# Taking the input tiles of the projection turned as well as plain, in a hybrid streaming encoder layer

## The chip, the cores and the metric

The kernel runs on one core of a Trainium2 chip. Its metric is the device time of one launch in microseconds (us). Time before: 3008.1 us, the median of three runs (3006.89 to 3008.73). The profile is of one execution, taken by the hardware profiler.

A core has a tensor engine (PE; its weight loads are listed as PEld), a vector engine (DVE), a scalar engine (ACT), a general engine (POOL), and a queue that issues most transfers (SP). Each works through its own queue in order, and they meet through semaphores. PE writes only to PSUM; DVE and ACT read it; POOL works on SBUF alone.

## The reference, cut to what matters

One layer on 2048 prompt rows and 128 sample rows of width 1024, 17 tiles of 128 rows in all, and on 256 memory rows (two tiles):

```
def rmsnorm(x, g):
    return x * rsqrt(mean(x * x, axis=-1) + EPS) * g

mk, mv = rmsnorm(mem, g_mem_kv) @ w_mk, rmsnorm(mem, g_mem_kv) @ w_mv   # memory keys and values
h = rmsnorm(x, g_mix_pre)
q, k, v, u_val, u_gate = split(h @ w_in)        # 1024 -> 5 x 512
att = band_attention(q, k, v);  c = conv_module(u_val * sigmoid(u_gate))
x = x + rmsnorm(concat(att, c) @ w_out, g_mix_post)
x = x + rmsnorm(memory_attention(rmsnorm(x, g_mem_pre), mk, mv), g_mem_post)
x = x + rmsnorm((silu(h2 @ w_gate) * (h2 @ w_up)) @ w_down, g_ffn_post)   # h2 = rmsnorm(x, g_ffn_pre)
```

The change concerns the first norm of x and the norm of the memory: a scale per row (a token), a weight per column (a channel), and then a product that contracts over the channels, for which the channels have to lie on the partitions.

## The kernel before, in words

All products are of float32 numbers cut into a high and a low half in a rounded format (`hi` is the cast, `lo` what is left), and each product is done as three: high by high, high by low, low by high (lines 288 to 290, `mm3`). So each weight tile of 128 x 1024 is loaded by SP (line 277), cast by ACT (line 281), and subtracted by DVE or POOL (line 283), through three load buffers and four pairs of halves.

The stages in order of time:

- *Memory stage* (`phase_mem`, up to about 111 us). Both memory tiles are normed, turned and split. Then, for the eight blocks of w_mk, 24 products of 256 columns each (the K product), with a pair of transposes per block to bring the result back (line 413); then a fold of w_mq into the keys, eight weights, 32 sums of six products, each sum copied out of PSUM by DVE (line 448) (called f1 below); then the eight blocks of w_mv (the V product); and a fold of w_mo into the values, 16 sums of six products of 512 columns, copied out at line 462 (f2).
- *Projection* (`phase_proj`, up to about 560 us). The 17 tiles are taken in three groups (`GROUPS`) of two sub-blocks of up to three tiles; per sub-block `norm_sub` norms, turns and splits its tiles into one of three pairs of buffers (`hh`, `hl`). Per group PE makes the gate and value inputs of the convolution (384 columns, line 510), then v (256 columns, line 660), then k and q. DVE runs the depthwise convolution between its other work (line 542), and POOL one quarter of it (line 552). The last products are followed by attention, the output projection, the memory attention and the feed-forward part, which the change leaves alone.

A tile's norm (`prenorm_halves`) is, before: SP loads the tile with rows on the partitions (line 500, or 385 for the memory), ACT squares it and sums each row (line 313), POOL makes the scale (lines 305 and 306), DVE multiplies the tile by the row's scale and the weight, which lies spread over all partitions (line 331), PE turns the eight blocks of 128 x 128 by transposes into two PSUM tiles (line 335), ACT casts each to the high half (line 337), and DVE subtracts (line 338). The tiles' load buffers (`xt`) are two. For the memory, PE spreads the weight over the partitions by two products with ones (line 398), among transposes of the identity that do nothing else (line 395).

The order on each engine isn't written out: a scheduler sets it when the program is built, from the order of the code, priorities and its own estimate of the times, and it lets a norm of a later tile pass other work where its buffers are free. So the norms of the projection's first tiles lie among the products of the memory stage. Most of PSUM is four sum tiles (`mm`) and two for transposes (`tr`).

## Time and profile before

| | us |
|---|---|
| median of three runs | 3008.1 |
| span of the profiled execution | 3000.1 |
| median less span | 8.0 |
| PE busy in the span | 2949.2 |
| DVE busy | 2134.6 |
| ACT busy | 1360.3 |
| POOL busy | 1416.7 |

The profile gives no launch time for the profiled execution itself; its span is 3000.1 us, from the first instruction to the last, and 8.0 us is what the median of the runs has beyond it. A row of a timeline has the start, the duration, the engine, the line of the kernel, the operation, what is written and read, and, in brackets, how long the engine was idle before and what it waited for. A row of a group has the busy time, the mean duration in ns, and the idle time ahead of it. Busy times of PE overlap, since its products are pipelined: the step from one start to the next tells what one costs.

### The profile page before, as it was taken

To read this page: it belongs to the slowest core of one execution; us is meant where nothing else is said; L and a number is where in the kernel's file an instruction comes from. 1 tells how busy PE (TensorE), PEld (TensorE's weight loads), DVE (VectorE), ACT (ScalarE), POOL (GpSimd) and SP (SyncE) were. 2 spreads that over 40 slices of the span, in tenths; PEclk is the share of its full clock that TensorE was granted. 3 is DMA by queue.
4 is the path that set the end of the run, shared out by engine and by line. 5 is a ranking of instruction groups with operands and counts; after the bars stand their busy time and mean duration, and the time that the engine had idled before them with its cause. 6 is when DMAs were issued, how large, how long until landed. Compare 5 with 4: busy or idle time off the path is not lost.

```text
span 3000.1 us, 46145 instructions
## 1 busy us (share of the span) xinstructions
PE 2949.2 (98%) x16940; PEld 2714.6 (90%) x16940; DVE 2134.6 (71%) x3090; ACT 1360.3 (45%) x2731; POOL 1416.7 (47%) x1338
## 2 busy tenths in 40 slices
PE   9999999999999999999999999999999999999998
PEld 9999999989997887887888999999999999888777
DVE  6687886968776466435358888888788998555666
ACT  5535455668883344323334333433344444433433
POOL 0267496721123244136357565446555775424413
PEclk9999999989999999999999999999999999999999
DMA  7645253664435456323246333544334336756664
GB/s 278 246 138 185 88 170 108 201 213 168 155 138 175 169 199 205 105 87 133 88 163 222 116 137 124 196 153 152 134 134 157 142 140 205 256 176 215 217 223 148
DMA packets 197552, 499.57 MB, mean 167 GB/s; under 512 B 19334, under 2 KB 84750, under 8 KB 188485
## 3 DMA queue, kind: packets, MB, share of 16 engines
q1 hardware_dynamic: 182397, 427.01, 41.9%
q0 software_dynamic: 14928, 69.61, 6.2%
q8 instruction: 133, 2.18, 0.3%
q14 instruction: 94, 0.77, 0.1%
HBM read 365.45 MB, written 141.81 MB: 169 GB/s over the span
## 4 chain that ended last, share of the span: by engine, by line
PE 38%; DMA 4%; issue 3%; DVE 3%; POOL 3%; ACT 0%; SPq 0%; DVEq 0%; POOLq 0%; ACTq 0%
PE psb L290 12%; PE psb L288 12%; PE psb L289 12%; DMA sbf<-in_w_down_dram 2%; POOL sbf L1569 1%; PE psb L296 1%; DMA sbf<-x 1%; PE psb L1424 1%; DMA sbf<-hn 0%; DVE sbr L1639 0%; DVE sbr L1447 0%; POOL sbf L346 0%; DVE sbr L1573 0%; DMA sbf<-in_w_gate_dram 0%; DVE sbx L1447 0%
## 5 line engine op out<-in xcount | busy, mean ns | idle before, releaser
L288 PE MATMUL psb<-sbr 128*128 128x384 f32 (+3 forms) x2808 | 941.7, 337 | 4.1 <-DVE sbx L676 1.6
L289 PE MATMUL psb<-sbr 128*128 128x384 f32 (+3 forms) x2356 | 804.6, 342 | 0.4 <-DVE sbr L338 0.3
L290 PE MATMUL psb<-sbr 128*128 128x512 f32 (+3 forms) x1848 | 633.1, 344 | 4.3 <-DVE sbr L1639 4.1
L288 PEld LDWEIGHTS psb<-sbr 128*128 128x128 f32 x2808 | 529.2, 189 | 34.6 <-ACT sbr L1638 2.8
L290 PE MATMUL psb<-sbr,sbx 128*128 128x384 f32 (+2 forms) x1484 | 475.8, 321 | 0.0
L289 PEld LDWEIGHTS psb<-sbr 128*128 128x128 f32 x2356 | 443.9, 188 | 27.1 <-DVE sbr L1427 0.7
L290 PEld LDWEIGHTS psb<-sbr 128*128 128x128 f32 x1848 | 347.9, 188 | 34.9 <-DVE sbr L1639 8.2
L296 PE MATMUL psb<-sbr 128*128 128x512 f32 x1200 | 295.3, 394 | 1.9 <-ACT sbr L1317 1.1
L1447 DVE TENSOR_TENSOR sbr<-sbf,sbr 128x512 fp32r<-128x512 f32 x258 | 262.7, 1021 | 38.8 <-ACT sbr L1446 37.9
L1446 ACT CAST sbr<-sbf 128x512 fp32r<-128x512 f32 x258 | 159.2, 620 | 277.4 <-PE psb L289 229.3
L290 PEld LDWEIGHTS psb<-sbr,sbx 128*128 128x128 f32 x1484 | 279.6, 189 | 0.2
L542 DVE SCALAR_TENSOR_TENSOR psb<-sbf,psb 128x768 f32<-128x768 f32 (+1 forms) x290 | 264.3, 911 | 6.1
L296 PEld LDWEIGHTS psb<-sbr 128*128 128x128 f32 x1200 | 222.2, 189 | 47.6 <-ACT sbr L1317 1.3
L1639 DVE TENSOR_TENSOR sbr<-sbf,sbr 128x384 fp32r<-128x384 f32 (+2 forms) x242 | 168.1, 717 | 99.2 <-ACT sbr L1638 98.0
L283 POOL TENSOR_TENSOR sbx<-sbf,sbr 128x1024 fp32r<-128x1024 f32 (+1 forms) x62 | 155.0, 2501 | 84.8 <-ACT sbr L281 81.0
L1638 ACT CAST sbr<-sbf 128x384 fp32r<-128x384 f32 (+2 forms) x242 | 112.4, 483 | 174.1 <-PE psb L289 149.8
L1569 POOL TENSOR_TENSOR sbf<-sbf 128x512 f32<-128x512 f32 x77 | 106.5, 1390 | 168.7 <-DMA sbf<-in_w_down_dram 167.1
L552 POOL TENSOR_TENSOR flexb<-flexb,flexb 128x128 f32<-128x128 f32 (+1 forms) x180 | 168.9, 939 | 25.4 <-ACT flexb L551 15.1
L288 PE MATMUL psb<-sbr,sbx 128*128 128x384 f32 (+1 forms) x524 | 170.6, 327 | 1.8 <-ACT sbx L1446 1.1
L1446 ACT CAST sbx<-sbf 128x512 fp32r<-128x512 f32 x153 | 94.7, 620 | 163.4 <-PE psb L289 143.4
L1447 DVE TENSOR_TENSOR sbx<-sbf,sbx 128x512 fp32r<-128x512 f32 x153 | 153.4, 1004 | 17.0 <-ACT sbx L1446 16.8
L1441 POOL TENSOR_TENSOR sbf<-sbf 128x512 f32<-128x512 f32 x66 | 97.5, 1477 | 107.2 <-DVE sbr L1447 50.7
(350 smaller groups left out, 6281.5 us busy)
## 6 DMA issues: line engine op xcount, KB each, us to landing
af<-flexb SPq DMA_DIRECT2D x33, 1344.0 KB, 5.8
sbf<-in_w_down_dram SPq DMA_DIRECT2D x154, 256.0 KB, 3.5
sbf<-in_w_gate_dram SPq DMA_DIRECT2D x66, 512.0 KB, 3.3
sbf<-in_w_up_dram SPq DMA_DIRECT2D x66, 512.0 KB, 3.5
sbf<-af SPq DMA_DIRECT2D x85, 384.0 KB, 4.3
sbf<-x SPq DMA_DIRECT2D x49, 512.0 KB, 3.8
sbf<-in_w_in_dram SPq DMA_DIRECT2D x48, 512.0 KB, 3.8
sbr<-ks POOLq DMA_DIRECT2D x16, 1024.0 KB, 8.6
```

What stands on the lines that cost most here:

```text
L283: self.lo_engine.tensor_tensor(lo[:, c], wf[:, c], hi[:, c].bitcast(F32), ALU.subtract)
L288: nc.tensor.matmul(ps, lh, rh, start=start, stop=False, **kw)
L289: nc.tensor.matmul(ps, lh, rl, start=False, stop=False, **kw)
L290: nc.tensor.matmul(ps, ll, rh, start=False, stop=stop, **kw)
L296: nc.tensor.matmul(y[o], l, r[:, o * 512:(o + 1) * 512], start=start and x == 0, stop=stop and x == 2)
L542: nc.vector.scalar_tensor_tensor(acc if w < CW - 1 else o, src(w), cwt[:, j, w:w + 1], acc, ALU.mult, ALU.add)
L552: nc.gpsimd.tensor_tensor(o, o, v, ALU.add)
L1446: nc.scalar.copy(hs[j][:, :], src[j])
L1447: nc.vector.tensor_tensor(ls[j][:, :], src[j], hs[j][:, :].bitcast(F32), ALU.subtract)
L1569: nc.gpsimd.tensor_tensor(acc[:, :], acc[:, :], q[:, :], ALU.add if s > 0 else ALU.subtract)
L1638: nc.scalar.copy(ch[:, m], a[:, x, m])
L1639: nc.vector.tensor_tensor(cl[:, m], a[:, x, m], ch[:, m].bitcast(F32), ALU.subtract)
```

## The change

The host now also passes x and the memory turned: for each tile, channels on the partitions, in eight blocks of 128 tokens. `prenorm_halves` is replaced by two functions, and the two norm weights come in with channels on the partitions, one number for each partition and block (`gT`).

```
--- before
+++ after
-    def prenorm_halves(self, pool, pspool, xt, gbc, hi, lo):
+    def row_scale(self, pool, natural, r):
         nc = self.nc
-        r = self.rms(pool, xt[:, :])
-        nc.vector.scalar_tensor_tensor(xt[:, :], xt[:, :], r[:, :], gbc[:, :], ALU.mult, ALU.mult)
+        xt = self.t(pool, [P, D], F32, "xt")
+        nc.sync.dma_start(xt[:, :], natural)
+        junk = self.t(pool, [P, D], BF16, "junk")
+        nc.scalar.activation(junk[:, :], xt[:, :], AF.Square, accum_out=r)
+        nc.gpsimd.tensor_scalar(r, r, 1.0 / D, EPS, ALU.mult, ALU.add)
+        self.last_pow = nc.gpsimd.tensor_tensor(r, r, self.mhalf[:, 0:1], ALU.pow)
+
+    def norm_turned(self, pool, pspool, turned, r, gT, hi, lo):
+        nc = self.nc
+        xT = self.t(pool, [P, KC, P], F32, "xT")
+        nc.sync.dma_start(xT[:, :, :], turned)
+        nc.gpsimd.tensor_tensor(xT[:, :, :], xT[:, :, :], gT[:, :].unsqueeze(2).to_broadcast([P, KC, P]), ALU.mult)
+        ps = self.t(pspool, [P, P], F32, "tr")
+        nc.tensor.transpose(ps[:, :], r.to_broadcast([P, P]), self.ident[:, :])
         for k0 in range(0, KC, 4):
-            ps = self.t(pspool, [P, 4, P], F32, "tr")
-            for k in range(4):
-                nc.tensor.transpose(ps[:, k, :], xt[:, (k0 + k) * P:(k0 + k + 1) * P], self.ident[:, :])
             sl = slice(k0, k0 + 4)
-            last = (nc.scalar.copy(hi[:, sl, :], ps[:, :, :]),
-                    nc.vector.tensor_tensor(lo[:, sl, :], ps[:, :, :], hi[:, sl, :].bitcast(F32), ALU.subtract))
+            nc.vector.tensor_tensor(xT[:, sl, :], xT[:, sl, :], ps[:, :].unsqueeze(1).to_broadcast([P, 4, P]), ALU.mult)
+            last = (nc.scalar.copy(hi[:, sl, :], xT[:, sl, :]),
+                    nc.vector.tensor_tensor(lo[:, sl, :], xT[:, sl, :], hi[:, sl, :].bitcast(F32), ALU.subtract))
...
-        for o in range(3):
-            with self.tc.issue_after(event.ins) if event else ExitStack():
-                for _ in range(WARM[o]):
-                    nc.tensor.transpose(warm[:, :], self.ident[:, :], self.ident[:, :])
-            if o < 2:
-                oc = slice(o * 512, (o + 1) * 512)
-                event = nc.tensor.matmul(gbc[:, oc], ones[:, :], gain[:, oc], start=True, stop=True)
+        for _ in range(WARM):
+            nc.tensor.transpose(warm[:, :], self.ident[:, :], self.ident[:, :])
...
             for i, t in enumerate(sub):
-                xt = self.t(pool, [P, D], F32, "xt", 2)
-                nc.sync.dma_start(xt[:, :], self.rows("x", t))
-                self.prenorm_halves(pool, ps_tr, xt, gbc, hh[:, :, i * P:(i + 1) * P], hl[:, :, i * P:(i + 1) * P])
+                self.norm_turned(pool, ps_tr, A["xT"][t], rx[:, t:t + 1], gT, hh[:, :, i * P:(i + 1) * P], hl[:, :, i * P:(i + 1) * P])
...
+        rx = self.t(pool, [P, NPT + 1], F32, "rx")
+
+        def scales(subs):
+            for sub in subs:
+                for t in sub:
+                    self.row_scale(pool, self.rows("x", t), rx[:, t:t + 1])
+
+        scales(GROUPS[0])
         nxt = [norm_sub(GROUPS[0][0]), norm_sub(GROUPS[0][1])]
         conv_halo()
+        scales(GROUPS[1])
...
+            if gi == 1:
+                scales(GROUPS[2])
```

So the plain tile now serves only for the row's scale, one column of a small tile (`rx`) per tile, taken for whole groups ahead. The turned tile is multiplied by the weight on POOL; one transpose of the scale, spread over 128 columns, puts the scales of the tile's tokens along the free dimension on all partitions; and DVE multiplies both halves of the tile by it, reading the scales from PSUM. ACT and DVE split the tile as before, but out of SBUF. The space of the old weight (4 KB) and one of the two plain buffers went to two buffers for turned tiles; plain tiles of the projection now pass through one buffer. For the memory tiles, the products with ones go, and the twelve transposes of the identity stand together. The intermediate `yf` of the memory stage moved to another place.

More of the change, by code (lines that the diff above doesn't have):

```diff
@@ L44 @@
 LATE = 5
-WARM = (6, 0, 6)
+WARM = 12
 HP = 100
@@ L174, in early @@
                    .lay(sbF, 2, ("thx", 2, 1), ("zx", 2, 2), ("xnx", 2, 2))
-                .lay(sbF, 44.75, ("us", 5.75, 1), ("cwt", 0.484375, 1), ("cvec", 0.0625, 1), ("half", 0.0625, 1))
+                .lay(sbF, 44.75, ("us", 5.75, 1), ("cwt", 0.484375, 1), ("cvec", 0.0625, 1), ("half", 0.0625, 1), ("gT", 0.03125, 1), ("rx", 0.09375, 1))
                    .lay(fb, 0, ("ct", 3, 5), ("bst", 0.03125, 2), ("bmv", 0.03125, 2), ("ss", 0.03125, 6),
@@ L469, in phase_proj @@
         big = [P, KC, 3 * P]
-        gbc = self.gain(pool, "g_mix_pre", "gbc")
+        gT = self.t(pool, [P, KC], F32, "gT")
+        nc.sync.dma_start(gT[:, :], A["g_mix_preT"])
         cwt = self.t(pool, [P, 4, CW], F32, "cwt", 1)
@@ L1682, in layout, with turned @@
     o["mem_prompt"] = i["mem_prompt"].reshape(NM, D)
+    def turned(x):
+        return x.reshape(-1, P, KC, P).transpose(0, 3, 2, 1)
+    o["xT"] = turned(np.concatenate([o["x_prompt"], o["x_sample"]]))
+    o["mem_promptT"] = turned(o["mem_prompt"])
+    for n in ("g_mix_pre", "g_mem_kv"):
+        o[n + "T"] = i[n].reshape(KC, P).T
     o["cache_att_k"] = i["cache_att_k"].reshape(DEC_B, PAST, 512)
@@ L1704, in layout @@
     o["w_down"] = i["w_down"].reshape(NF, P, D)
-    for n in ("g_mix_pre", "g_mix_post", "g_mem_pre", "g_mem_post", "g_mem_kv", "g_ffn_pre", "g_ffn_post"):
+    for n in ("g_mix_post", "g_mem_pre", "g_mem_post", "g_ffn_pre", "g_ffn_post"):
         o[n] = i[n].reshape(D)
```

22 lines of the change are left out of this document (8 added, 14 removed).

## The prediction

> **What bounds the kernel now.** I read the page first, then stretches of the first 490 us (all that the change touches), then PE's waits there.
>
> ```profile
> PE 2949.2 (98%) x16940; PEld 2714.6 (90%) x16940; DVE 2134.6 (71%) x3090; ACT 1360.3 (45%) x2731; POOL 1416.7 (47%) x1338
> ```
> ```profile
> 13.00:37.50 24.50, 24.31 (x204) 24.31 (x205) 17.85 (x26) 14.57 (x30) 0.00 (x0) 1.00 0.69 243
> 37.50:60.30 22.80, 22.80 (x192) 22.74 (x191) 18.81 (x37) 8.32 (x12) 0.00 (x0) 1.00 0.92 315
> 60.30:86.00 25.70, 25.70 (x218) 25.70 (x217) 18.25 (x29) 15.31 (x30) 2.32 (x4) 1.00 0.71 248
> 86.00:111.00 25.00, 25.00 (x124) 20.70 (x123) 23.15 (x34) 14.34 (x25) 5.52 (x6) 1.00 0.90 324
> 111.00:150.00 39.00, 38.65 (x237) 37.93 (x236) 19.49 (x23) 18.62 (x36) 16.67 (x17) 1.00 0.54 201
> 150.00:490.00 340.00, 338.45 (x2192) 337.31 (x2191) 261.99 (x322) 160.32 (x261) 236.36 (x162) 1.00 0.43 143
> ```
> ```profile
> PE psb L288 <- DVE sbx L676: 1.6, 2, 0.8
> PE psb L335 <- DVE sbr L338: 0.5, 1, 0.5
> ```
>
> Columns of the stretches: length, then busy time (and instructions) of PE, PEld, DVE, ACT, POOL, then granted clock, DMA share, GB/s. The rows are the memory stage (K product, f1, V product, f2), the start of the projection, and the projection. PE hardly pauses from 13 us on, at clock 1.00, so a product that leaves PE's queue shortens the run by its issue time, unless its place becomes a wait. Two stretches have little room: DMA is at 0.92 in f1, and DVE is busy 23.15 of 25.0 us in f2.
>
> Sums go against the profiled execution: span 3000.1 us, 8.0 us under the 3008.1 us median of the runs; I keep those 8.0.
>
> **The change part by part.**
>
> *Transposes.* Per tile eight go and one comes: 152 become 19.
>
> ```profile
> 114.37 0.33 PE L290 MATMUL psb<-sbr,sbx 128*128 128x384 f32 x1
> 114.54 0.34 PE L288 MATMUL psb<-sbr 128*128 128x384 f32 x1
> 114.72 1.03 PE L335 MATMUL psb<-ident,sbf 128*128 128x128 f32 x8
> 115.51 0.42 PE L289 MATMUL psb<-sbr 128*128 128x384 f32 x1
> 115.77 0.34 PE L290 MATMUL psb<-sbr,sbx 128*128 128x384 f32 x1
> ```
>
> Products issue every 0.17 us. From 114.54 to 115.77 two issue steps (0.35) and the block of eight passed: 1.23 - 0.35 = 0.88 us, 0.11 each. Seven fewer per tile save 0.77 us; for the 17 tiles of x **13.1 us**. The memory's two tiles lie ahead of the first product and are counted below.
>
> *Start.* Two gain products (L398) and the scale of the whole row go; two turned loads and two POOL products come.
>
> ```profile
> 4.43 1.06 ACT L313 ACTIVATE sbf<-sbf 128x1024 bf16<-128x1024 f32 x1 [2.43 <-DMA sbf<-in_mem_prompt_dram]
> 5.83 1.06 ACT L313 ACTIVATE sbf<-sbf 128x1024 bf16<-128x1024 f32 x1 [0.25 <-DMA sbf<-in_mem_prompt_dram]
> 12.45 1.37 DVE L338 TENSOR_TENSOR sbr<-psb,sbr 128x512 fp32r<-128x512 f32 x2 [0.97 <-ACT sbr L337]
> 13.19 0.38 PE L289 MATMUL psb<-sbr 128*128 128x256 f32 x1 [0.34 <-DVE sbr L338]
> ```
> ```profile
> L346 POOL TENSOR_TENSOR sbf<-sbf 128x1024 f32<-128x1024 f32 x16 | 40.4, 2522 | 11.7 <-DVE sbf L345 11.7
> ```
>
> Natural loads land 1.4 us apart; without the gain's issue in front (0.4) at 4.0 and 5.4, so the first turned tile at about 7.0 (estimate, one more step of 1.4 and the small gain). POOL multiplies two tiles, 2.5 us each by L346, the same size: 9.5, 12.0. DVE then does the second tile's two halves (1.3) and three subtractions up to the one that the second kind of product waits for (2.0): 15.2, against 13.19. I take **+2.0**, with ends +1.0 (turned tile at 6.0) and +3.5 (at 8.5). The first weight lands later too, behind two more loads, but POOL takes its low half only after the two tiles, so it is not later than that.
>
> *DVE, ACT, POOL per tile.*
>
> ```profile
> L338 DVE TENSOR_TENSOR sbr<-psb,sbr x38: 676/683/692, 9.9 to 465.0; 128x512 fp32r<-128x512 f32 x38
> L331 DVE SCALAR_TENSOR_TENSOR sbf<-sbf,flexb x17: 1275/1285/2864, 70.9 to 425.0; 128x1024 f32<-128x1024 f32 x17
> ```
>
> DVE had 1.28 + 2 x 0.68 = 2.65 us; now four of 0.68, 2.7 us: nothing. ACT keeps one square and two casts. POOL gains 2.5 us per tile, 28 us for tiles 6 to 16, on top of 236 in 340 us: hidden, as weights are prepared up to four ahead. If that cover went, each of these low halves would come 2.5 us late.
>
> L331 reads SBUF twice and was stretched to 2.86 us; L338 reads PSUM and never was, and its successor reads SBUF twice. The Trainium skill, SBUF — State Buffer, section Who interferes with whom, says that such a DVE operation and a POOL operation exclude each other for the whole instruction; by the stretched row the trace agrees. By the unstretched rows the extra cost is nothing; by that rule 22 subtractions in the projection would each wait about 1 us on average (estimate), 22 us on a DVE that idles 78 us there, and I would add 1 us: 3002.6 in place of 3001.6.
>
> *Projection.* The 0.35 us before 150 us and the 1.6 us behind L676 may go, or grow through a DVE queue that now also waits for POOL's product. I take **+1.0**, ends -1.5 and +3.
>
> *f1: a new wait in PE's queue.* The scale's transpose writes one of two PSUM halves, which is free when DVE has multiplied the tile before last. In the order in which the changed program is built, the tiles pass as 1, 3, 5 and then 0, 2, 4; PE meets the transpose of tile 5 in f1, after 19 of its 32 sums; it waits for DVE on tile 3, whose turned load goes into tile 1's buffer, freed after the 7th sum.
>
> ```profile
> 42.42 0.42 DVE L448 COPY flexb<-psb 128x256 f32<-128x256 f32 x1 [0.29 <-PE psb L290]
> 43.14 0.43 DVE L448 COPY flexb<-psb 128x256 f32<-128x256 f32 x1 [0.29 <-PE psb L290]
> ```
> ```profile
> 92.44 0.40 SPq L500 DMA_DIRECT2D sbf<-in_x_prompt_dram  x1
> 97.61 1.06 ACT L313 ACTIVATE sbf<-sbf 128x1024 bf16<-128x1024 f32 x1 [3.75 <-DMA sbf<-in_x_prompt_dram]
> 98.57 0.19 ACT L313 ACTIVATION_READ_ACCUMULATOR sbf<-sbf 128x1 f32 x1
> 100.22 0.33 SPq L500 DMA_DIRECT2D sbf<-in_x_prompt_dram  x1
> 107.69 1.06 ACT L313 ACTIVATE sbf<-sbf 128x1024 bf16<-128x1024 f32 x1 [0.94 <-DMA sbf<-in_x_prompt_dram]
> ```
>
> A sum takes 0.72 us. Counted from f1's start: buffer free at 7 x 0.72 = 5.0, plus about 2.3 for tile 1's halves in DVE's queue, 7.3; landing 5.2 later (92.44 to 97.61), 12.5; POOL 2.5, 15.0; DVE 1.3, 16.3. PE is there at 19 x 0.72 = 13.7. **+2.5**; ends 0 (landing within 2.6) and +5 (landing 7.5, as from 100.22 to 107.69). Behind it stand PE's whole queue and, in DVE's, four evictions.
>
> *f2.* PE sheds 24 transposes (2.6 us) and would leave after 22.4 us, but DVE's work there stays near 23.2, and tile 2's turned load, needed for the first projection, now starts only when tile 0 is done in the same stage. **+1.0**, ends 0 and +4.
>
> *Queues and DMA.* SP issues 19 more loads of 512 KB at 0.33 us: hidden. Natural loads of tiles 0 to 5 now stand between the weight loads of the K product and f1, through one buffer: each waits in SP's queue for ACT's square of the one before, and two or three weights pass between two of them. PE uses a weight in 24 products of 0.12 (13.53 to 13.65) and one pair of transposes, about 3.1 us, two in 6.2. A round is landing + 1.06 + 0.19 + about 0.3 for the handoff: 6.0 to 6.8 with landings of 4.4 to 5.2.
>
> ```profile
> 13.53 0.28 PE L288 MATMUL psb<-sbr 128*128 128x256 f32 x1
> 13.65 0.28 PE L289 MATMUL psb<-sbr 128*128 128x256 f32 x1
> 18.11 1.23 DVE L283 TENSOR_TENSOR sbx<-sbf,sbr 128x1024 fp32r<-128x1024 f32 x1 [1.35 <-ACT sbr L281]
> ```
> ```profile
> sbf<-in_w_mqT_dram SPq DMA_DIRECT2D x8, 512.0 KB, 4.4
> ```
>
> So it just keeps up. The lead: the fourth weight is ready at 19.3 (18.11 + 1.23) and used at 13.2 + 3 x 3.1 = 22.5, 3.2 us; its load waits for the first weight's low half, which POOL ends 3.2 us later than now (15.0 against 11.8, estimate), and PE starts 2.0 later: about 2 us are left. I take **0.1**, ends 0 and the fourth case below.
>
> *Sum.* 13.1 - (2.0 + 1.0 + 2.5 + 1.0 + 0.1) = 6.5: span 2993.6, median **3001.6 us**.
>
> **The rivals.**
>
> *A, the forecast:* the saving, half given back: 3001.6, own range 2998 to 3003.
>
> *B, covered:* nothing is late behind the start (PE paused nowhere in the memory stage, which speaks for it): 13.1 - 2.0 = 11.1, 2997.0. Against it: the queue order above.
>
> *C, given back:* loads land in 7.5 us, not 5.2, with DMA at 0.9 and nine more loads before 60 us. The wait in f1 grows by 2.3, tile 2 comes 2.3 later: 3006.2. For it: 107.69; against it: 97.61 and the median 4.4.
>
> *D, slower:* the chain of natural loads starves the weights. The opening stretch had a 512 KB load that landed in 8.5 us.
>
> ```profile
> sbf<-in_g_mix_pre_dram SPq DMA_DIRECT2D x1, 512.0 KB, 8.5
> ```
>
> With that the round is 10.05, 3.85 more than PE's 6.2, in five rounds 19 us, less the lead of 2: 3001.6 + 17 = 3018.6. It turns the sign past the bound (12.5 above the forecast) when a round exceeds 9.1 us, a landing of 7.6.
>
> The Trainium skill, DMA: Bandwidth & Descriptors, section Anatomy of one DMA, fits a transfer as 2.0 us and its bytes at 436 GB/s: 3.2 us for 512 KB, so by that rule a round of 4.8 never starves PE and B is right; the landings of this trace are longer, and they decide.
>
> **How the numbers follow.** A measurement tells about 0.2% (6 us) from no change. A 0.36, B 0.12, C 0.32, D 0.20. Faster by more than 0.2%: A and B less the upper edge of A, 0.46; within: 0.34; slower: D, 0.20. Range 2995 to 3013: B's case and 2 us of before's small waits below, C and the beginnings of D above.
>
> **What would show it.** Transposes at the new line: 19, and about 0.1 us each between products. First steady product near 15.2 us. PE's waits before 130 us: one on DVE's scale product of 2 to 3 us in f1, about 1 at the end of f2, none on ACT's weight cast. DVE's subtraction with minimum 0.68 and a longer maximum. From 600 us on PE's stretches as before, 6 us earlier. Wrong if PE waits for weights in the K product (D), if the wait in f1 is under 0.5 (B) or over 4 (C), or if the projection pauses for more than 3 us.

## The result, and the profile after

The changed kernel took 3024.5 us (median of 4 runs, 3023.2 to 3027.5), the kernel before 3007.5 us beside it (median of 4, 3006.8 to 3008.7): a ratio of 1.0067, 95% interval 1.0048 to 1.0087. It is slower; 3001.6 was forecast, with 3013 as the upper end.

The profiled execution of the changed kernel has a span of 3023.5 us and took 3025.3, so only 1.8 us lie around a span. The 8.0 us that the prediction put around the span of the kernel before were mostly something else: by the same 1.8 us its profiled execution took some 3001.9 us (estimate), less than any of the four runs beside the changed kernel. So the two profiles differ by 23.4 us and the medians by 17.0; the some 6 us between are that one execution of the kernel before, not the change. A second profile of the kernel before (an experiment, below) has a span of 3000.5 at a time of 3002.3, on a chip where the median of that kernel is 3002.0; so whether the first was a short execution or on such a chip is not known.

First row: the page of the changed kernel, busy time and instructions per engine. Then its waits of PE in the first 620 us (us in total, times, longest; a short one at the very start is left out).

```profile
PE 2941.6 (97%) x16803; PEld 2706.8 (90%) x16803; DVE 2148.2 (71%) x3108; ACT 1359.8 (45%) x2731; POOL 1451.7 (48%) x1357
```
```profile
PE psb L288 <- ACT sbr L348: 6.2, 1, 6.2
PE psb L288 <- DVE sbx L686: 6.0, 3, 4.7
PE psb L289 <- DVE sbx L283: 3.7, 1, 3.7
PE psb L344 <- POOL sbf L335: 3.0, 2, 2.1
PE psb L344 <- DVE sbf L347: 1.9, 1, 1.9
...
PE psb L288 <- ACT sbr L281: 1.0, 1, 1.0
PE psb L289 <- DVE sbr L349: 0.7, 1, 0.7
```

The profile counts 137 instructions of PE less (133 transposes and two products went) and 7.6 us less of busy time; the time went into waits that the kernel before did not have or had shorter: the first product (L348), v's evictions (L686), the weight split on DVE at the end of f2 (L283), a tile's transpose in f1 (L347), and the transposes of the two memory tiles ahead of the first product (L335, at 6.3 and 7.7 us).

Where the time went is read from the same landmarks in both traces, in us from the start of the span: the starts of the first and last eviction of f1 (line 448) and of the last of f2 (line 462), the first glu (the first gated input of the convolution, which DVE writes at line 625 before and 633 after), the last subtraction for k in the projection (line 714 before, 724 after; so the projection runs on to some 615 us, not 560), the last score product of attention, and the end. The third row is the difference; the forecast is the sum of the prediction's own steps up to there, with 0.77 us per tile taken off where the kernel before turned its tiles (5 of 17 ahead of the first glu, 12 behind it).

| | f1 first | f1 last | f2 last | first glu | projection's end | last score | end |
|---|---|---|---|---|---|---|---|
| before | 38.6 | 61.5 | 111.2 | 120.3 | 614.6 | 896.4 | 3000.1 |
| after | 44.8 | 71.3 | 125.8 | 134.3 | 625.1 | 920.4 | 3023.5 |
| later by | +6.2 | +9.8 | +14.6 | +14.0 | +10.5 | +24.0 | +23.4 |
| forecast | +2.0 | +4.5 | | +1.6 | -6.5 | -6.5 | -6.5 |

So of the 30 us between forecast and end 17 lie ahead of the projection's end, and 13.5 inside attention, whose code is the same in both.

**The start.** PE's rows of the changed kernel at its first products, then two stretches of it (columns as in the prediction; the x number is the instructions), then POOL and DVE ahead of them.

```profile
14.30 0.58 PE L288 MATMUL psb<-sbr 128*128 128x256 f32 x1 [6.16 <-ACT sbr L348]
15.85 0.58 PE L288 MATMUL psb<-sbr 128*128 128x256 f32 x1 [0.96 <-ACT sbr L281]
17.14 0.58 PE L289 MATMUL psb<-sbr 128*128 128x256 f32 x1 [0.71 <-DVE sbr L349]
```
```profile
17.00:22.00 5.00, 4.86 (x22) 4.86 (x23) 2.96 (x4) 0.80 (x2) 4.03 (x3) 1.00 0.89 341
22.00:27.00 5.00, 5.00 (x41) 5.00 (x41) 2.78 (x4) 3.62 (x7) 2.84 (x4) 1.00 0.62 228
```

```profile
9.13 3.75 POOL L342 TENSOR_TENSOR sbf<-sbf 128x1024 f32<-128x1024 f32 x2 [1.52 <-DMA sbf<-in_mem_promptT_dram]
14.11 3.58 DVE L349 TENSOR_TENSOR sbr<-sbf,sbr 128x512 fp32r<-128x512 f32 x4
```

POOL waited for the first turned tile up to 9.13 us, and of DVE's four subtractions from 14.11 on the first took 1.77 us, beside a weight split of POOL. PE stood still for 6.2 us, and then made 22 instructions in 5 us where later it makes 41: its products step by 0.21 us up to 22.4 us and by 0.12 behind that. (The clock column says 1.00 there because the profile's first record of the clock is later, at 22.6 us; in the kernel before it is at 12.2 us.)

**The end of f2.** DVE and POOL of the changed kernel.

```profile
113.95 1.78 DVE L349 TENSOR_TENSOR sbr<-sbf,sbr 128x512 fp32r<-128x512 f32 x1
115.66 3.36 DVE L283 TENSOR_TENSOR sbx<-sbf,sbr 128x1024 fp32r<-128x1024 f32 x1
```
```profile
112.92 2.27 POOL L342 TENSOR_TENSOR sbf<-sbf 128x1024 f32<-128x1024 f32 x1 [5.96 <-DVE flexb L462]
115.15 2.78 POOL L283 TENSOR_TENSOR sbx<-sbf,sbr 128x1024 fp32r<-128x1024 f32 x1
```
```profile
119.08 0.79 PE L289 MATMUL psb<-sbx,sbr 128*128 128x512 f32 x1 [3.69 <-DVE sbx L283]
```

A weight split takes DVE 1.21 to 1.23 us elsewhere; this one ends 1.1 us after POOL's split ends at 117.93, and the subtraction ahead of it 0.55 us after POOL's product ends at 115.19. So each looks as if it stood still until POOL was done, which is tested below. PE waits 3.69 us for it. In the kernel before no split on DVE took more than 1.23 us.

**The clock.** Stretches of the changed kernel around that wait and around the 4.7 us wait in the v products.

```profile
118.10:124.90 6.80, 5.82 (x14) 4.57 (x15) 5.66 (x9) 1.42 (x3) 4.72 (x2) 0.50 0.77 258
125.00:131.00 6.00, 6.00 (x35) 5.83 (x35) 3.42 (x3) 2.10 (x2) 4.24 (x2) 1.00 0.99 363
220.50:227.30 6.80, 6.06 (x28) 6.06 (x29) 3.35 (x6) 1.81 (x4) 4.64 (x3) 0.50 0.66 212
227.40:233.40 6.00, 5.70 (x47) 5.46 (x47) 6.00 (x9) 4.33 (x8) 2.51 (x2) 1.00 0.49 161
```

With each of the two waits PE's granted clock falls to 0.50 for 6.8 us; half of the 5.8 and 6.1 us in which PE worked at it, some 3 us, is what that costs (estimate). In the kernel before it is 1.00 from its first record to 623 us. The wait of 1.9 us in f1 has no such stretch behind it. The Trainium skill, TensorE: Matmul & The Clock Gate, section Part 1: The HAM clock gate, says that an idle window of some 3.4 us halves the clock and that a busy one gives it back, in windows that run freely. The traces agree on the windows: in each profile of this study all changes of the clock lie on a grid of 3.41 us (stretches of 3.4, 6.8, 10.2 us). They do not agree that a whole window has to be idle. Up to 615 us, over the 17 profiles, half clock followed each of the 23 grid intervals at full clock in which PE stood idle for 2.0 us or more, and 2 of the 25 with 1.2 to 1.9 us. So a wait's place on the grid decides, and not its length alone. Two of the kernels below show it, the best version and the one with attention's loads behind the last norm, with PE's row behind the wait and then the clock:

```profile
111.33 0.61 PE L290 MATMUL psb<-sbx,sbr 128*128 128x512 f32 x1 [2.10 <-DVE sbx L284]
111.60:115.00 3.40, 3.40 (x9) 2.62 (x9) 3.40 (x7) 0.39 (x1) 2.94 (x2) 0.50 0.72 245
```
```profile
120.28 0.50 PE L289 MATMUL psb<-sbx,sbr 128*128 128x512 f32 x1 [3.67 <-DVE sbx L283]
118.40:125.20 6.80, 4.53 (x20) 3.49 (x21) 6.80 (x10) 3.32 (x4) 5.60 (x4) 1.00 0.77 270
```

The first wait, 2.1 us, lies in one interval and is followed by half clock; the second, 3.7 us, falls into two intervals, 1.8 and 1.9 us, and is followed by none.

**Attention.** The kernel before, then the changed one: the store of the third of five late convolution norms on SP, POOL's loads for head 1 (4 MB), and ACT at the fifth norm, which needs the third one's buffer (two buffers).

```profile
637.75 0.32 SPq L578 DMA_DIRECT2D cs<-sbf  x1
...
638.73 0.64 POOL L853 DMA_DIRECT2D sbr<-qs  x1
639.37 1.22 POOL L855 DMA_DIRECT2D sbr<-ks  x2
640.41 0.73 POOL L856 DMA_DIRECT2D sbr<-vs  x1
...
641.70 1.51 ACT L573 ACTIVATE sbf<-psb,sbf 128x128 f32<-128x128 f32 x4 [0.56 <-PE psb L570]
```
```profile
648.35 0.64 POOL L863 DMA_DIRECT2D sbr<-qs  x1
648.99 1.21 POOL L865 DMA_DIRECT2D sbr<-ks  x2
650.03 0.72 POOL L866 DMA_DIRECT2D sbr<-vs  x1
...
650.31 1.79 SPq L577 DMA_DIRECT2D cs<-sbf  x2
...
663.95 1.50 ACT L572 ACTIVATE sbf<-psb,sbf 128x128 f32<-128x128 f32 x4 [9.58 <-DMA cs<-sbf]
...
665.51 2.08 PE L901 MATMUL psb<-ident,flexb 128*128 128x128 f32 x7 [7.84 <-ACT sbf L572]
```

In the kernel before the store leaves 1.0 us ahead of the 4 MB, and the fifth norm does not wait for it 4.0 us later (its landing is not recorded; that of the second store, 3.5 us earlier, took 2.2 us). In the changed kernel it leaves 2.0 us behind the first of these loads and lands in 13.6. ACT waits 9.58 us with casts behind it in its queue, PE 7.84 us, and the clock is at 0.50 for 23.9 us there instead of 20.5. Softmax number 10 of attention (from 0) comes 1.5 us earlier than before, counted from the first score product, number 12 comes 14.6 us later: 16.0 us at one place.

### The profile page after: what moved, and what is told of

The parts are those of the page before. It is cut to its first block, busy times and chain, and to the rows that moved or that the text cites. A ratio compares the mean times of both kernels' runs of the same rounds, so it can differ in the third digit from the quotient of the medians.

```text
span 3023.5 us, 45902 instructions
## 1 busy us (share of the span) xinstructions
PE 2941.6 (97%) x16803; PEld 2706.8 (90%) x16803; DVE 2148.2 (71%) x3108; ACT 1359.8 (45%) x2731; POOL 1451.7 (48%) x1357
## 4 chain that ended last, share of the span: by engine, by line
PE 40%; DMA 3%; DVE 3%; POOL 3%; issue 2%; ACT 1%; SPq 0%; DVEq 0%; POOLq 0%; ACTq 0%
PE psb L290 12%; PE psb L289 12%; PE psb L288 12%; PE psb L296 2%; DMA sbf<-in_w_down_dram 1%; POOL sbf L1579 1%; DMA sbf<-x 1%; PE psb L1434 1%; DVE sbr L1649 1%; POOL sbf L357 0%; DVE sbr L1457 0%; DVE sbf L374 0%; DMA sbf<-in_w_gate_dram 0%; DVE sbr L1583 0%; DVE sbx L1457 0%
## 5 line engine op out<-in xcount | busy, mean ns | idle before, releaser
L283 POOL TENSOR_TENSOR sbx<-sbf,sbr 128x1024 fp32r<-128x1024 f32 (+1 forms) x62 | 148.7, 2399 | 52.4 <-ACT sbr L281 51.1
L1457 DVE TENSOR_TENSOR sbx<-sbf,sbx 128x512 fp32r<-128x512 f32 x153 | 153.7, 1006 | 15.4 <-ACT sbx L1456 15.2
```

What stands on the lines that cost most here:

```text
L283: self.lo_engine.tensor_tensor(lo[:, c], wf[:, c], hi[:, c].bitcast(F32), ALU.subtract)
L1457: nc.vector.tensor_tensor(ls[j][:, :], src[j], hs[j][:, :].bitcast(F32), ALU.subtract)
```

## The experiments

The theory after these readings, T in the expectations: the loss is the start (first product later, then half clock), DVE's standstill beside POOL, the v products' wait, and one late store in attention, each with half clock behind it. Its rivals, R, stand with each run. Ratios are to the kernel before beside it; a difference of 0.001 is 3 us. "Later by" is against the first profile of the kernel before.

**How far one program's profiles differ.** The kernel before again, unchanged.

> The kernel before once more, unchanged, for a second profile: how far stages differ between executions of one program. If the stages up to the first glu differ by under 1 us between its two profiles, lags of 2 us and more there belong to the change; attention's length (279.3 us in the first profile from the first to the last score product) tells what of the 13 us lost there can be chance.

Every landmark up to the projection's end lies within 0.1 us of the first profile, the last score 2.2 us later, the end 0.4. For the changed kernel that is not so. Three of the kernels below (attention's loads behind the last norm, a third buffer, the bias tables earlier) have its order on every engine, the first two up to attention, the third up to 129 us. Their lags beside its own, and the start of the steady run of products:

| | steady run from | f1 first | f1 last | f2 last | first glu | projection's end |
|---|---|---|---|---|---|---|
| the changed kernel | 17.1 | +6.2 | +9.8 | +14.6 | +14.0 | +10.5 |
| loads behind the last norm | 16.0 | +4.4 | +10.7 | +13.8 | +13.7 | +12.6 |
| a third buffer | 16.1 | +4.8 | +8.8 | +11.5 | +11.1 | +7.3 |
| bias tables earlier | 16.3 | +5.2 | +10.3 | +15.1 | | |

So a difference of under 2 us at f1, or of 3 to 5 us up to the projection's end, between two kernels with turned tiles can be that of two executions. The wait of 3.7 us at the end of f2 is in all four, with the same durations of 1.78 and 3.36 us on DVE; the half clock with it lasts 6.8, 0, 0 and 3.4 us.

**Attention's loads behind the last norm.**

```diff
-            self.late_event = self.last_pow
...
-            nc.vector.scalar_tensor_tensor(z[:, :, :], th[:, :, :], 1.0, z[:, :, :], ALU.add, ALU.mult)
+            self.late_event = nc.vector.scalar_tensor_tensor(z[:, :, :], th[:, :, :], 1.0, z[:, :, :], ALU.add, ALU.mult)
```

> The changed kernel, with one instruction as the event behind which attention's loads of head 1 (q, k and v, 4 MB on POOL's queue) are issued: the last convolution norm's final multiply by DVE in place of its rstd on POOL, so that no store of a convolution norm shares the DMA engines with those 4 MB. Theory T (the 13 us lost in attention are one late store: it landed after 13.6 us instead of 2.2, held ACT by 9.6 us and PE by 7.8 us, and PE then ran at half clock): the PE wait on ACT of 7.8 us is gone, the long stretch at half clock shrinks by some 7 us, the time falls by 8 to 11 us, to 3013 to 3017. Rival R (the loss only moves on: head 1's loads now come later and its first score waits for them, or the next buffer does): another PE wait of 5 us or more between 630 and 720 us, time 3021 to 3027.

3023.7 us, ratio 1.0052 (1.0038 to 1.0067). PE's 7.8 us wait went to 1.5, but ACT still waited 4.2 us for the store, which now stood beside two loads of 512 KB, and from softmax 10 to 12 it lost 9.2 us instead of 16.0. T's place was right, its gain was not reached: the edit took away one neighbour of the store, not the wait for it.

**A third buffer.** What the store holds up is a buffer, so one more was given (2 KB that were free).

```diff
-                   .lay(sbF, 2, ("thx", 2, 1), ("zx", 2, 2), ("xnx", 2, 2))
+                   .lay(sbF, 2, ("thx", 2, 1))
+                   .at("zx", 2, (sbF, [4, 6, 0])).lay(sbF, 8, ("xnx", 2, 2))
```

> The changed kernel with three buffers in place of two for the result of the late convolution norms (zx), so that the fifth norm need not wait for the store of the third, which lands late when attention's 4 MB for head 1 are being fetched. Between the 10th and the 12th softmax of attention the changed kernel lost 16 us against the kernel before, and so did every kernel in which ACT waited 7.7 us or more for that store (the changed one, the one with earlier bias tables, the memory half alone, the product on ACT); the four without that wait lost under 3.5 there. Theory T: ACT's wait for the store is gone, the loss at the 12th softmax is under 4 us, the time is 8 to 12 us below the changed kernel's: ratio to the kernel before 1.001 to 1.003. Rival R (the planner's order, not the store, sets that place): the loss stays over 8 us, ratio 1.004 to 1.007.

Ratio 1.0035 (1.0022 to 1.0049), 0.0032 or 9.6 us below the changed kernel's; span 3013.6, 9.9 less. PE's waits between 620 and 700 us in that kernel, longest group first:

```profile
PE psb L885 <- DVE flexb L797: 4.0, 4, 1.6
PE psb L570 <- DVE sbf L566: 1.4, 1, 1.4
PE psb L902 <- ACT sbf L573: 1.2, 1, 1.2
```

The wait on ACT is 1.2 us instead of 7.8, and from softmax 10 to 12 the loss is 2.7 instead of 16.0. T holds for that place: its loss is the wait for the store. Not all of the 13.5 us in attention go with it. Of the 9.9 us of span 3.2 lie ahead of the projection's end, where the order is the changed kernel's; from there to the last score this kernel still loses 7.0 us, 6.6 less. The wait is not tied to the turned tiles: of the kernels with two buffers, the four in which ACT waited 7.7 us or more for it lost 15.6 to 16.8 us at this place (the changed kernel, and of the kernels below the ones with the bias tables earlier, the memory half alone and the weight on ACT), those in which it waited 3.2 and 4.2 us at a time lost 8.2 and 9.2 (the scaled tile in PSUM, attention's loads behind the last norm), and those in which it waited 1.3 us or less lost 2.7 to 3.0 (PE kept busy, eight transposes, the projection half alone). As far as these kernels show, the order that the scheduler plans for attention decides, and it moves with changes ahead of it; why it comes out one way or the other was not tried.

**The bias tables earlier.** The call moves from behind the four glu blocks of group 0 into the first.

```diff
+                if gi == 0 and j == 0:
+                    self.bias_tables(Region().lay(fa, 0, ("fb", 3, 1), ("rv", 1, 1)), glu)
...
-            if gi == 0:
-                self.bias_tables(Region().lay(fa, 0, ("fb", 3, 1), ("rv", 1, 1)), glu)
```

> The changed kernel with the attention bias tables (and their 2.5 MB transfer) built behind the first of the four glu blocks of the first group instead of the fourth, some 60 us earlier, away from the v products. Theory T (the 4.7 us wait of PE in the v products comes from v's stores, which landed in up to 13.7 us beside that transfer, and costs another 3.4 us by the 6.8 us at half clock behind it): no PE wait above 1.5 us and no half clock between 195 and 240 us, time 6 to 8 us lower, 3016 to 3019. Rival R (the wait belongs to the row scales' natural loads ahead in SP's queue, which stay where they are): the wait stays at 4 to 5 us, time 3022 to 3027.

In the changed kernel v's stores and the table's transfer meet; the answers on transfers between 190 and 232 us have, as median from issue to landing:

```profile
toep<-fd POOLq DMA_DIRECT2D x1, 2560.0 KB, 17.4
vs<-sbx SPq DMA_DIRECT2D x8, 256.0 KB, 3.2
```

and the slowest of the eight stores took 13.7 us. With the tables earlier PE's longest wait there was 3.4 us (4.7 in the changed kernel, 5.6 and 3.8 in the two with its order), a stretch of 6.8 us at half clock remained, and the projection's end came 9.6 us later than before. Ratio 1.0047 (1.0033 to 1.0060): T's 6 to 8 us did not come, and that the transfer is a part of that wait is not shown. In the two kernels whose projection is as before, the kernel before and the memory half alone (below), v's evictions hold PE for 1.6 and 1.9 us in two waits each: the long wait comes with the projection's turned tiles, by a path that was not followed.

**PE kept busy before the first product.**

```diff
+        for _ in range(44):
+            nc.tensor.transpose(warm[:, :], rm[:, 1:2].to_broadcast([P, P]), self.ident[:, :])
```

> The changed kernel with 44 more 128x128 transposes of a row scale into a spare PSUM tile right behind the second memory tile's own, in the 6.2 us in which PE stood still before the first product. Theory T (the first 8 us of products ran at half clock because PE had stood still): products take 0.12 us from the first on, the first eviction of the f1 stage comes 3 to 4 us earlier (41 us instead of 44.8), time 3 to 4 us lower, 3020 to 3022. Rival R (the K product waits for its weights' landings and casts at that point anyway, the pace is set by them): first eviction at 44 to 45 us, time within 1.5 us of the changed kernel's.

The first f1 eviction came at 43.2 us (44.8 in the changed kernel, 43.0 to 43.9 in the three with its order, 38.6 before). Stretches of 13 to 20 us, this kernel and then the kernel before:

```profile
13.00:20.00 7.00, 6.08 (x52) 5.84 (x51) 6.29 (x8) 4.02 (x7) 4.50 (x6) 1.00 1.01 360
```
```profile
13.00:20.00 7.00, 6.81 (x57) 6.81 (x58) 5.40 (x8) 3.64 (x6) 0.00 (x0) 1.00 0.86 315
```

PE runs at full pace from the first product, which itself came at 14.5 us. Counted from it, the first f1 eviction follows 28.7 us later, 29.9 to 30.5 in the four profiles without the edit, and 26.1 in the kernel before: 1.2 to 1.8 us came back, not 3 to 4, and the larger part of the start's loss is not the clock's. The time, 3010.6 us or 1.0009 (0.9998 to 1.0020), fell by far more than the edit explains: this kernel's planned order has no late store in attention (2.7 us lost at that place), and f2 ended 7.9 us late instead of 11.5 to 15.1.

**Eight transposes instead of one.**

```diff
+        for _ in range(8):
-        nc.tensor.transpose(ps[:, :], r.to_broadcast([P, P]), self.ident[:, :])
+            nc.tensor.transpose(ps[:, :], r.to_broadcast([P, P]), self.ident[:, :])
```

> The changed kernel with the one transpose per tile issued eight times into the same PSUM tile (119 more over 17 tiles). My prediction's term: 0.77 us per tile, 13.1 us in all: time 3036 to 3039. Rival R (a transpose is hidden where PE waits at the tile's place, in 9 of the 17 tiles): 5 to 8 us, 3029 to 3033. The first 2 to 4 tiles (the start, where PE waits for data) should cost nothing in either.

(They are 133 more over 19 tiles, the memory's two included.) Ratio 1.0038 (1.0024 to 1.0052), less than the changed kernel's: again no late store (3.0 us lost there). Up to the projection's end it lies 18.7 us behind the kernel before, against 10.5, 12.6 and 7.3 in the three profiles of the changed kernel's order: 6 to 11 us, which does not part T from R. It was measured again without the store, below.

**Each half alone.** First the memory as before and the projection's 17 tiles turned; then the memory turned and the projection as before (the functions and calls of the one half put back).

> The memory tokens as in the kernel before (normalised, then eight transposes per tile), the projection's 17 tokens tiles less 0 as in the changed kernel: one half of the change alone. Theory T (each half pays its own part: the start 6.4 us, f1 to the first glu another 8 us which belong to the projection's tiles, then a gain of about 0.5 us per tile, then chance in attention): first f1 eviction as before, 49.8 +- 0.5 us in the trace's own count against 56.2; first glu 7 to 9 us behind the kernel before; time 3 to 8 us above the kernel before without a late store in attention, 12 to 16 with one. Rival R (the start is all of it, by the clock): first glu within 2 us of the kernel before, time at or below it.

> The memory tokens as in the changed kernel, the 17 tiles of the projection as in the kernel before: the other half alone. Theory T: first f1 eviction 5 to 7 us late, no further loss up to the first glu (5 to 7 us late), 5 to 8 us above the kernel before at the end. Rival R (the late start lets other work catch up, so that it is regained in f1 and f2): under 3 us.

(49.8 and 56.2 in the first are counted from 11.1 to 11.4 us ahead of the span.) The projection half: 2996.6 us, ratio 0.9985 (0.9976 to 0.9994), faster than the kernel before; its first f1 eviction was 3.1 us late and its first glu 9.8, its projection's end 6.2. T had about the right lag at the first glu (7 to 9), put the first f1 eviction as before, and had the wrong sign of the whole; the profile is of an execution of 3002.8 us. The memory half: 3012.1 us, 1.0036 (1.0023 to 1.0049); first f1 eviction 4.2 us late, first glu 4.7, each a little under T's 5 to 7, projection's end 5.1, and a late store in attention on top (ACT waited 9.4 us), so the time tells no more than the sum.

**The norm weight on ACT instead of POOL.**

```diff
-        nc.gpsimd.tensor_tensor(xT[:, :, :], xT[:, :, :], gT[:, :].unsqueeze(2).to_broadcast([P, KC, P]), ALU.mult)
+        for k in range(KC):
+            nc.scalar.activation(xT[:, k, :], xT[:, k, :], AF.Copy, scale=gT[:, k:k + 1])
```

> The changed kernel with the product by the norm weight on ACT (eight activations of 128x128 with a column of the weight as scale, some 3 us a tile) in place of one product on POOL (1.9 us). Theory T (DVE's instructions that read two SBUF operands stand still while POOL's product or subtraction of two SBUF operands runs: the subtraction L349 took up to 2.88 us instead of 0.69 and was lengthened by 18.8 us over 38, the weight split L283 once by 2.1, and the 3.7 us wait of PE at 115 us is that): no L283 on DVE above 1.3 us in f2, L349's total lengthening at most half (POOL's weight splits stay in the projection), the PE wait at the end of f2 under 2 us, 2 to 4 us less lag at the first glu. Rival R (the wait is DVE's queue, whose order stays): the wait stays at 3 us or more, and ACT's 57 us more make the time equal or longer than the changed kernel's.

PE's wait on DVE's split fell from 3.7 to 1.5 us, as T said. The first glu came 11.4 us late instead of 14.0, which lies within the 11.1 to 14.0 of the changed kernel's own order. The subtractions still summed to 40.2 us (43.8 in the changed kernel; 38 at 0.69 are 26): most of the lengthening stayed without POOL's products, and T's half was wrong. Ratio 1.0054 (1.0041 to 1.0067).

**The scaled tile in PSUM.** DVE's multiply writes PSUM, so that its subtraction has one operand in SBUF.

```diff
+            ps = self.t(pspool, [P, 4, P], F32, "tr")
-            nc.vector.tensor_tensor(xT[:, sl, :], xT[:, sl, :], ps[:, :].unsqueeze(1).to_broadcast([P, 4, P]), ALU.mult)
-            last = (nc.scalar.copy(hi[:, sl, :], xT[:, sl, :]),
-                    nc.vector.tensor_tensor(lo[:, sl, :], xT[:, sl, :], hi[:, sl, :].bitcast(F32), ALU.subtract))
+            nc.vector.tensor_tensor(ps[:, :, :], xT[:, sl, :], rs[:, :].unsqueeze(1).to_broadcast([P, 4, P]), ALU.mult)
+            last = (nc.scalar.copy(hi[:, sl, :], ps[:, :, :]),
+                    nc.vector.tensor_tensor(lo[:, sl, :], ps[:, :, :], hi[:, sl, :].bitcast(F32), ALU.subtract))
```

(Cut to what matters: `rs` is the spread scale, in two spare pieces of PSUM of 0.5 KB.)

> The changed kernel with DVE's multiply by the row scales written to PSUM instead of back to SBUF, so that ACT casts from PSUM and DVE's subtraction has one operand in SBUF instead of two. The same instructions otherwise. Theory T (a DVE instruction with two SBUF operands stands still while POOL reads SBUF for its product or its weight split; in the changed kernel 15 of 38 subtractions were lengthened, by 18.8 us together): no subtraction above 0.9 us, lengthening in all under 1 us. Up to the first glu 1 to 3 us gained, since the weight split on DVE at the end of f2 (3.36 us instead of 1.21) keeps its two SBUF operands. Attention by chance with or without the late store: time 3020 to 3024 with, 3008 to 3013 without, on a chip where the kernel before takes 3007. Rival R (the lengthening is contention for SBUF in general or a slow operand): the subtractions stay lengthened, some above 1.5 us.

The subtraction's durations (least, median, greatest in ns) in the changed kernel, and in this one:

```profile
L349 DVE TENSOR_TENSOR sbr<-sbf,sbr x38: 671/693/2878, 14.1 to 475.1; 128x512 fp32r<-128x512 f32 x38
```
```profile
L350 DVE TENSOR_TENSOR sbr<-psb,sbr x38: 673/682/695, 12.2 to 474.4; 128x512 fp32r<-128x512 f32 x38
```

No subtraction is stretched any more, as T said: two operands in SBUF beside a working POOL are what did it. The weight split at the end of f2, which keeps two operands in SBUF, still took 3.42 us, and PE waited 2.1 us for it instead of 3.7. That time was saved is not shown: the first glu came 10.9 us late, beside 11.1 to 14.0 in the changed kernel's order, and from f1's end to the first glu the kernel lost 3.6 us, where that order lost 2.2 to 4.2. At the start PE has new waits of 4.7 us on the multiply and 2.8 behind it, in place of the 6.2. Ratio 1.0021 (1.0007 to 1.0035), with a shorter wait of ACT for the store (4.3 us in two).

**The best version.** The memory as before, the projection turned, the multiply into PSUM, the third buffer; then the earlier bias tables as well.

> The memory tokens as in the kernel before, the projection's tiles as in the changed one with the multiply into PSUM and three buffers for the late convolution norms: the half that gained (0.9985 of the kernel before), without DVE's standstills. Theory T: 1 to 4 us below that half alone, ratio 0.997 to 0.9985; subtractions at 0.7 us; no wait of ACT for a norm's store. Rival R (DVE's lengthened instructions were off the path outside f2): ratio 0.998 to 0.9995, as that half alone.

> The same with the attention bias tables behind the first glu block instead of the fourth, away from the v products. Theory T (in the half alone PE waits 5.0 us for v's evictions and runs 6.8 us at half clock there): another 3 to 6 us less than the kernel without that edit. Rival R (as in the changed kernel, where the same edit left a wait of 3.4 us and moved the time by under 3 us): within 2 us of it.

2993.7 us, ratio 0.9972 (0.9961 to 0.9983), and 2992.7 us, ratio 0.9968 (0.9956 to 0.9979), the fastest kernel of the study: 8.6 us below the kernel before beside it. T's size for the first is right. The tables gave 1.0 us of median and not T's 3 to 6; at the projection's end of the profile it is 2.0 us ahead of the kernel before, against 2.8 behind, but 2.1 of these 4.8 us lie ahead of the first glu, before the tables. Its largest waits of PE up to 620 us:

```profile
PE psb L290 <- DVE sbx L284: 2.1, 1, 2.1
PE psb L289 <- DVE sbx L714: 1.5, 1, 1.5
PE psb L289 <- ACT sbr L364: 1.5, 1, 1.5
```

**What the version owes to what.** The kernel before with the third buffer and the earlier tables; the best version with the memory turned too; the best version with eight transposes per tile.

> The kernel before with the two edits that are no part of the change: three buffers for the late convolution norms, bias tables behind the first glu block. Theory T (in the kernel before neither the store nor v's evictions held PE for more than 1.6 us, so there is nothing to gain): ratio 0.999 to 1.001, so the 0.32% of the best version are the projection's turned tiles. Rival R (the gain is the two edits): ratio 0.9965 to 0.998.

> The changed kernel, memory tokens turned too, with the three edits of the best version (multiply into PSUM, third buffer, earlier bias tables). Against that version it differs by the memory half alone, with no late store in attention. Theory T (the memory half costs what its late first product and PE's half clock cost, 4 to 6 us up to the first f1 eviction, and gives nothing back): 4 to 8 us above the best version, ratio 0.998 to 1.0. Rival R (the 10 us of the memory half alone were the late store, the start is regained later): within 2 us of the best version, ratio 0.996 to 0.9975.

> The best version with each of its 17 transposes issued eight times, 119 more. My prediction's term, 0.11 us each on PE's path, gives 13.1 us: ratio 1.000 to 1.002. Rival R (hidden where PE waits at the tile's place, 6 of 17 tiles): 7 to 9 us, ratio 0.9985 to 1.000.

The kernel before with the two edits: ratio 0.9983 (0.9973 to 0.9992), between T and R. So about half of the best version's gain is the two edits, and the turned projection gives the other half, some 0.0015 or 4.5 us; but the two intervals overlap. Without these edits, in the half alone, the turned projection is below the kernel before by its whole interval (0.9976 to 0.9994). With the memory turned: 1.0004 (0.9996 to 1.0013), 0.0036 or 10.8 us above the best version, more than T's 4 to 8; in the profile the first product came 3.1 us later, the first f1 eviction 5.3, the projection's end 6.9. With eight transposes: 1.0024 (1.0013 to 1.0036), 0.0056 or 16.8 us above, just past T's range and far from R; in the profile 11.2 us at the projection's end and 13.4 in the span. The step in its timeline:

```profile
256.35 0.34 PE L290 MATMUL psb<-sbr 128*128 128x384 f32 x1
256.53 1.04 PE L360 MATMUL psb<-ident,sbf 128*128 128x128 f32 x8
257.32 0.42 PE L291 MATMUL psb<-sbr,sbx 128*128 128x384 f32 x1
```

From 256.35 to 257.32 lie one step of a product (0.18) and the eight: 0.79 us, 0.10 each.

## Why the prediction was wrong

*Transposes, 13.1 us saved:* right. Seven transposes more per tile cost 13.4 us of span in the best version, 11.2 of them by the projection's end. What removing them gains in the projection is a little less: 12 tiles by 0.77 are 9.2 us. From the first glu to the projection's end the best version gains 9.2, but the kernel before gains 2.2 there by the two edits alone, and the version without the earlier tables gains 6.5: 6.5 to 7.0 us for the turned tiles.

*Start, +2.0:* the mechanism was right and the size was not. The first product came at 14.3 us against 12.5, and the steady run, which the prediction put at 15.2 against 13.19, began at 17.14 behind two more waits (0.96 and 0.71): +3.95, past the upper end of 3.5; in the three profiles with the same order it is +2.8 to +3.1. Two terms were mis-sized. POOL could begin on the first turned tile at 9.13 us, not 7.0 (at 7.97 with attention's loads behind the last norm), though its two products took 3.75 us in all and not 5.0. And the three subtractions took 3.0 us instead of 2.0, the first of them 1.77 beside POOL's weight split. From there PE went on at half pace for some 5 us, which the step had not: 22 instructions where 41 fit, 19 by 0.12 or 2.3 us. The two make the 6.2 us by which the first f1 eviction was late; keeping PE busy gave 1.2 to 1.8 us back.

*f1, +2.5:* right in kind and near in size. The wait on DVE's multiply came at 1.9 us, where the prediction put it (2.2 and 1.7 us in the two profiles with the same order up to attention). f1 took 3.6 us longer in this profile; the next largest wait in it is one of 0.2 us on an eviction, and the rest was not followed.

*f2, +1.0, and DVE at no cost:* wrong, by a rule that the prediction had and priced at 1 us. From f1's end to the first glu the kernel lost 4.2 us (3.0 and 2.2 in the two profiles with the same order) where the steps gave a gain of 2.9. The subtraction lost its PSUM operand and stood still beside POOL, and so did the weight split behind it; PE's wait was 3.7 us in all four profiles, and the half clock with it cost some 3 us in this one and nothing in two others. With the subtraction in PSUM the loss here stayed at 3.6 us, so how much of it is the subtraction's standstill and how much the split's is open. The Trainium skill, SBUF — State Buffer, section Who interferes with whom, says that a DVE instruction with two SBUF inputs contends with one of GpSimd (POOL here) that reads SBUF; by that rule the trace agrees in both directions, up to 2.88 us with two, at most 0.695 with one. The error was to spread it over the projection, where DVE has room, and not to put it in f2, which the prediction itself showed as the stretch without room (23.15 of 25.0).

*Projection, +1.0:* too small, and past its upper end of +3. The steps gave a gain of 8.2 us there; 3.5 came, and 1.1 and 3.8 in the two profiles with the same order. The wait of 4.7 us for v's evictions (5.6 and 3.8 there) and some 3 us of half clock stand against it. The prediction had named a pause of more than 3 us in the projection as a sign of being wrong.

*Natural loads, +0.1:* right. No wait of PE for a weight's cast in the K product beyond 1.0 us at the start; rival D did not come, and B and C had the wrong places. (The fit that the prediction takes for B from the Trainium skill, DMA: Bandwidth & Descriptors, section Anatomy of one DMA, is given there for transfers that GpSimd issues; these loads are issued by SP, so it says nothing for B here.)

*From 600 us on as before, 6 us earlier:* wrong, and the largest single miss. Attention lost 13.5 us, and PE's and ACT's long waits in it are for one store; with the third buffer 6.6 of the 13.5 are gone (the whole kernel gains 9.6 us by the ratios). Nothing in the steps could give it, since the prediction took code that is not changed as time that is not changed; but the scheduler plans the whole program, and a store 1.0 us ahead of 4 MB of loads was 3 us away from where it meets the wait.

*The sum:* it went against a median 8.0 us above the span, of which some 6 were the profiled execution. That moved the forecast's zero, not its steps.

Still open: why the memory half costs 10.8 us of median when the profile shows 6.9 by the projection's end; what makes v's evictions late; differences of 4 us and more between kernels in the later heads of attention, the 7.0 us left with the third buffer among them; and which part of the planner's estimate turns the late norms' order.

## What to carry to other kernels

Price a wait of a tensor engine that is otherwise full with the half clock that may follow it: here the same wait of 3.7 us cost some 3 us more in one execution and nothing more in two, and a wait of 2.1 us could bring it too. When an operand moves from PSUM to SBUF, look for the engine that shares SBUF with the one that reads it, in the stretch with the least room, not on average. Where a scheduler orders the program, a transfer that leaves 1 us ahead of a large one can end up behind it by an edit elsewhere; one more buffer behind it was worth 0.0032 of the time here. And before a lag of a few us between two kernels is read as the edit's, look for kernels with the same order there: here they differed by up to 3 us at the first glu.

## What the runs showed of the hardware

- The granted clock changed on a grid of 3.41 us. Half clock followed all 23 full-clock intervals with 2.0 us or more of idle PE, and 2 of 25 with 1.2 to 1.9 us: so a wait of 2.1 us could halve it, and one of 3.7 us, split over two intervals, left it at 1.00. In 6.8 us at half clock PE made 28 instructions around the v products, in 6.0 us behind them 47.
- A store of 256 KB landed in 13.6 us beside 4 MB of loads of which the first was issued 2 us ahead of it, where another store of that size in the kernel before landed in 2.2; with those loads moved away it still took 6.1 us beside two loads of 512 KB, and kept ACT for 4.2.
- POOL's product with a column spread over the tokens took 1.89 us (the least of 19, with a median of 1.90) where its subtraction of two full tiles of that size takes 2.40 (median); the prediction took 2.5.
